# Residual rows kept in DRAM, and a second standing buffer for modulation weights

## The chip, the cores and the metric

The kernel runs on one core of a Trainium2 chip. A core has a matrix engine (TensorE, PE in the profile), a vector engine (VectorE, DVE), a scalar engine (ScalarE, ACT), a general engine (GpSimd, POOL) and SyncE (SP), which here issues nearly all the DMAs; 16 DMA engines move data between DRAM and the core's SBUF memory of 128 partitions. Each engine runs its own list of instructions in order and waits on semaphores for the others. The metric is the device time of one execution in microseconds, as a median of runs.

## The reference

One inference step of a small flow-matching backbone: 384 tokens (128 of context, 256 latent) by 1024 channels go through four layers. Layer `l` has the mixer `l mod 3`: a bidirectional state-space scan (SSD) in layers 0 and 3, a gated short convolution in layer 1, differential attention in layer 2. Each mixer and each conv-FFN (1024 to 5632, gated to 2816, back to 1024) stands between two norms, and its result is added to the residual `x`:

```
def sandwich_layer(x, mod, g, mix_fn, ffn_fn):
    sh1, sc1, gt1, sh2, sc2, gt2 = jnp.split(mod, 6, axis=-1)
    m, aux = mix_fn(rmsnorm(x, g[0]) * (1 + sc1) + sh1)
    x = x + gt1 * rmsnorm(m, g[1])
    f = ffn_fn(rmsnorm(x, g[2]) * (1 + sc2) + sh2)
    x = x + gt2 * rmsnorm(f, g[3])
    return x, aux
```

`mod` is `silu(c) @ w_mod[l]` plus a bias, with one vector `c` for latent and one for context tokens, and a `w_mod[l]` of 24 MB in each layer. The result is float32; the kernel splits each factor of its large products into a high and a low part and makes three matmuls of each.

## The kernel before

**Phases.** The program is unrolled. For each layer: the mixer, with activations held channel-major (channels on partitions); the mixer's output projection, token-major, in `tm_out`; the FFN's up projection (L374 holds the matmuls of all channel-major projections) with convolution and gate; the FFN's down projection, again in `tm_out` (matmuls at L414). A `tm_out` makes three row tiles of 128 tokens (t0, t1, t2), and works in two halves of 512 output columns. At the end of its second half each row tile is finished in turn: `gated` takes the projection times its gate, `residual` (L355) adds it to `x`, `normed` makes `xn`, `turned` transposes it on PE (L291), and `modulated` makes `hh` and `hl`, which the next phase's matmuls read. That end is called a turn here; there are eight: A and B behind mixer and FFN of layer 0, C and D of layer 1, E and F of layer 2, G and H of layer 3. In a turn PE has little left to do but transposes, and the chain goes through DVE, ACT and POOL for each row tile.

**Residual.** `x` is three tiles of 128 x 1024 float32 (512 KB each, 4 KB of a partition), in a pool of their own (`xp`), loaded once at the start by `tokens` and updated in place.

**Modulation.** The product with `w_mod` is cut into 24 units a layer, 96 in all. A unit loads a block of 1 MB and runs matmuls of it into `modps` (L184); eight units end in `mod_finish`, which adds the bias row `brow` on DVE (L194, L195), transposes (L198) and, for the gates, stores them to DRAM (`gd`). Units are fill work: `pace` puts them into all phases by a table of how many are to be done by when, and `need` forces those that a phase reads. Their blocks lie in `wm`, a standing buffer (`WM` of them) in the weights' pool, and in `wx`, of which `room` many lie in a phase's own pool: 7 at the start, 4 in the turns of the short convolution and of attention, 1 in the other `tm_out`, 0 elsewhere. `stock` issues the loads for all free buffers, `modbuf` picks the buffer, and `fill` runs units:

```
    def fill(self, n, stock=99):
        for _ in range(n):
            if self.filler:
                self.stock(stock)
                self.filler.pop(0)[1](self.modraw.pop(0)[0])
```

**Other loads.** Weights come in chunks of 512 KB (`wr`, 4 buffers), are split by ACT and DVE into `wh` and `wl` (4 buffers), and are thus some chunks ahead of PE. `gates` (L63 in the trace) reads a gate back from `gd`, spread over all partitions, at the middle of a `tm_out`.

**Order.** The Tile framework schedules the instructions of each engine statically, with a simulated timeline, and sets the semaphores. All loads and stores named here go through SP in one order; a DMA whose buffer isn't free, or whose source isn't ready, holds those behind it. DMAs rotate over eight semaphores, so that one waits for the eighth before it. A pool that is opened for a phase takes the memory of the phase before, and its tiles wait for the readers of what lay there.

Of the kernel before, what the change touches and what calls it, by code (L numbers as in the profile page):

```python
# [10 lines left out]
F32 = mybir.dt.float32  # L11
# [8 lines left out]
P = 128  # L20
D = 1024
KB = D // P
# [4 lines left out]
NF = FFN // P  # L27
# [4 lines left out]
EPS = 1e-6  # L32
# [3 lines left out]
WS = 4  # L36
WM = 1
RB = 7
# [6 lines left out]
class Net:  # L45
    def __init__(self, ctx, tc, d, layers):
        self.tc, self.nc, self.d, self.layers = tc, tc.nc, d, layers
        pool = lambda name, bufs=1, **kw: ctx.enter_context(tc.tile_pool(name=name, bufs=bufs, **kw))
        self.cp = pool("const")
        self.xp = pool("x")  # L50
        self.hp = pool("h")
        self.wp = pool("w", 3)
        self.mp = pool("mod", 1)
        self.sm = pool("small", 4)
        self.dp = pool("dram", 1, space=DRAM)
        self.pt = pool("pt", 2, space=PSUM)
        self.pm = pool("pm", 1, space=PSUM)
        self.V, self.S, self.GP, self.PE = self.nc.vector, self.nc.scalar, self.nc.gpsimd, self.nc.tensor
        self.consts()
# [42 lines left out]
    def tokens(self, lo, hi):  # L102
        d = self.d
        for t in range(lo, hi):
            xt = self.xp.tile([P, D], F32, name=f"x{t}")
            self.load(xt, d["x_prompt"] if t == 0 else d["x_sample"][(t - 1) * P:t * P, :])
            self.x.append(xt)

# [245 lines left out]

    def residual(self, t, parts, eps=EPS):  # L355

        r = self.rstd(parts[t, 0][1], parts[t, 1][1], eps)
        out = []
        for hf, xs in enumerate(self.halves(self.x[t])):
            self.V.scalar_tensor_tensor(xs, parts[t, hf][0], r, xs, op0=ALU.mult, op1=ALU.add)  # L360
            out.append(self.sums(xs))
        return out

# [21 lines left out]
    def tm_out(self, *args, room, **kw):  # L385

        with self.tc.tile_pool(name="out", bufs=1, reuse_waits="tile") as self.op:
            self.room, self.hbufs = room, HB
            self.stock()
            self._tm_out(*args, **kw)  # L390
            self.room = 0

    def _tm_out(self, l, gate, nk, prep, eps=None, then=None):
        self.goal["turn"] = self.goal["mid"] if gate == 0 else self.goal["end"]
        self.need(l, gate + 1)
        parts = {}
        self.limit = self.wpos + nk
        for hf in range(2):
# [6 lines left out]
            for k, t in order:  # L405
# [9 lines left out]
                if hf == 1 and k == nk - 1:  # L415
                    self.gated(t, 1, acc[t], gt, parts)
                    ss = self.residual(t, parts, EPS if eps is None else eps[t])
                    then(t, ss)
                    self.pace("turn", t + 1, NT)
# [23 lines left out]
    def run(self):  # L443
        tc = self.tc
        self.modres, self.filler, self.modraw, self.room = {}, [], [], 0
        self.x = []
        self.wplan = [c for l in self.layers for c in self.plan(l)]
# [47 lines left out]
    def ffn(self, l, pl, then):  # L495
        d = self.d
# [20 lines left out]

        self.tm_out(l, 1, NF, prep, then=then, room=1)

    def short(self, l, pl, then):  # L520
        d = self.d
# [5 lines left out]
        for i in range(KB):  # L527
# [7 lines left out]
            t = self.conv(cg, cw[:, i])  # L535
            self.V.tensor_tensor(t, pb, t, op=ALU.mult)
            self.split(t, hi[i], lo[i])
            self.pace("mix", i + 1, KB)
        self.tm_out(l, 0, KB, lambda k: (hi[k], lo[k]), then=then, room=4)

    def ssd(self, l, pl, then):
# [26 lines left out]

        self.tm_out(l, 0, 16, prep, eps=eps, then=then, room=1)

# [231 lines left out]
    def attn(self, l, pl, then):  # L802
        oh = [pl.tile([P, 2, T], F32R, name=f"oh{i}") for i in range(4)]
        ol = [pl.tile([P, 2, T], F32R, name=f"ol{i}") for i in range(4)]
        with self.tc.tile_pool(name=f"heads{l}", bufs=1, reuse_waits="tile") as hp:
            self.attn_core(l, hp, oh, ol)
        self.tm_out(l, 0, KB, lambda k: (oh[k // 2][:, k % 2, :], ol[k // 2][:, k % 2, :]), then=then, room=4)

# [250 lines left out]
```

## Time and profile before

| | us |
|---|---|
| median of 3 runs | 2415.24 (2411.56 to 2415.72) |
| the profiled execution | 2410.85 |
| its span | 2409.03 |
| PE busy | 2291.4 (95%) |
| DVE busy | 1613.2 (67%) |
| ACT busy | 1248.5 (52%) |
| DMA, mean share of its 16 engines | 48.8% |
| mean clock granted to PE | 0.975 |

A time of the trace counts from the start of the span. The granted clock is a share of 2.4 GHz: 1.0 or, at its lower level of 1.2 GHz, 0.5; a value between is a mean over a stretch. The stages, from the windows of the trace: start 0 to 43, mixer of layer 0 to 343, its projection and turn A to 437, FFN of layer 0 to 626, turn B to 733, layer 1's mixer to 845, turn C to 901, FFN to 1084, turn D to 1191, attention to 1346, turn E to 1444, FFN to 1629, turn F to 1737, layer 3's mixer to 2039, turn G to 2124, FFN to 2310, turn H to the end.

### The profile page before, as it was taken

The page shows a single profiled execution, that of the slowest core. Times are in us where ns is not written, and L with a number is a line of the kernel's source. Part 1 is how long each engine was busy: PE and PEld are TensorE (multiplying, and loading weights), DVE is VectorE, ACT ScalarE, POOL GpSimd, SP SyncE. Part 2 cuts the span into 40 slices and gives each one's busy share as a digit, 9 for nine tenths or more (in the row PEclk, how much of TensorE's full clock was granted, in tenths as well). Part 3 has the DMA queues.
Part 4 walks back from the last instruction along what each step waited for, and adds up shares of the span by engine and source line. Part 5 has one row for each costly group of instructions (what it writes and reads, how often), then busy time and mean ns, then how long its engine had stood idle before and what let it go on. Part 6 is the DMA issues. An engine that isn't in the chain of part 4 may idle for free.

```text
span 2409.0 us, 35648 instructions
## 1 busy us (share of the span) xinstructions
PE 2291.4 (95%) x13132; PEld 2001.4 (83%) x13132; DVE 1613.2 (67%) x2928; ACT 1248.5 (52%) x2165; POOL 330.0 (14%) x498
## 2 busy tenths in 40 slices
PE   6989999899999999999999979999898999989998
PEld 3878887799877959998788649998687888789987
DVE  3888786677655467776645547776578888677765
ACT  3766675444453344445544444445566676554444
POOL 1222221100000010000223320000113223110000
PEclk8999999999999999999999989999999999989999
DMA  7665655533547563335434453344465654423342
GB/s 293 188 173 206 213 189 177 201 123 124 165 135 292 194 246 116 131 123 164 157 123 153 153 236 109 131 129 157 141 171 168 190 178 143 131 98 125 130 147 80
DMA packets 113375, 391.79 MB, mean 163 GB/s; under 512 B 13105, under 2 KB 25521, under 8 KB 100913
## 3 DMA queue, kind: packets, MB, share of 16 engines
q1 hardware_dynamic: 113200, 389.52, 48.8%
q8 instruction: 103, 1.69, 0.3%
q14 instruction: 72, 0.58, 0.1%
HBM read 382.39 MB, written 7.08 MB: 162 GB/s over the span
## 4 chain that ended last, share of the span: by engine, by line
PE 81%; DVE 8%; DMA 4%; issue 2%; ACT 2%; POOL 2%; SPq 0%; DVEq 0%; POOLq 0%; ACTq 0%
PE mm L374 46%; PE mm L414 20%; PE mm L846 5%; PE modps L184 3%; PE yp L414 2%; DVE e L719 2%; PE yp L759 2%; DMA wm<-in_w_mod 1%; DVE wl L153 1%; PE yp L887 1%; DVE w L723 1%; DMA h<-in_state 1%; DMA wx<-in_w_mod 1%; PE yp L374 1%; ACT jk L260 1%
## 5 line engine op out<-in xcount | busy, mean ns | idle before, releaser
L374 PE MATMUL mm<-hh,wh 128*128 128x384 f32 (+1 forms) x2352 | 795.9, 340 | 11.3 <-DVE cv L434 7.4
L374 PE MATMUL mm<-hl,wh 128*128 128x384 f32 (+1 forms) x2352 | 794.7, 338 | 1.8 <-POOL hl L346 1.8
L374 PE MATMUL mm<-hh,wl 128*128 128x384 f32 (+1 forms) x2352 | 791.5, 338 | 0.0
L153 DVE TENSOR_TENSOR wl<-wr,wh 128x1024 fp32r<-128x1024 f32 (+2 forms) x466 | 564.9, 1214 | 278.6 <-ACT wh L152 277.9
L152 ACT ACTIVATE wh<-wr 128x1024 fp32r<-128x1024 f32 (+2 forms) x466 | 483.4, 1039 | 340.7 <-PE mm L374 261.6
L374 PEld LDWEIGHTS mm<-hh,wh 128*128 128x128 f32 (+1 forms) x2352 | 442.7, 189 | 37.3 <-DVE cv L434 11.4
L374 PEld LDWEIGHTS mm<-hl,wh 128*128 128x128 f32 (+1 forms) x2352 | 442.6, 188 | 5.8 <-POOL hl L346 2.3
L374 PEld LDWEIGHTS mm<-hh,wl 128*128 128x128 f32 (+1 forms) x2352 | 442.4, 188 | 5.0 <-issue 3.1
L430 ACT ACTIVATE cv<-mm,fcw 128x384 f32<-128x384 f32 x176 | 100.1, 571 | 233.3 <-PE mm L374 228.2
L414 PE MATMUL mm<-wh,gh 128*128 128x512 f32 x528 | 208.7, 395 | 0.0
L414 PE MATMUL mm<-wl,gh 128*128 128x512 f32 x528 | 208.6, 395 | 0.0
L414 PE MATMUL mm<-wh,gl 128*128 128x512 f32 x528 | 207.9, 395 | 0.0
L432 DVE SCALAR_TENSOR_TENSOR cv<-mm,fcw,cv 128x127 f32<-128x127 f32 x352 | 144.3, 411 | 42.5 <-ACT cv L430 42.5
L439 ACT ACTIVATE gh<-fg 128x384 fp32r<-128x384 f32 x176 | 92.2, 524 | 152.5 <-PE mm L414 151.6
L268 POOL TENSOR_SCALAR m<-s 128x1 f32<-128x1 f32 x42 | 17.1, 406 | 1123.3 <-ACT jk L260 1122.4
L440 DVE TENSOR_TENSOR gl<-fg,gh 128x384 fp32r<-128x384 f32 x176 | 97.6, 557 | 96.7 <-ACT gh L439 96.1
L434 DVE SCALAR_TENSOR_TENSOR cv<-mm,fcw,cv 128x127 f32<-128x127 f32 x352 | 146.0, 416 | 10.9
L414 PEld LDWEIGHTS mm<-wh,gh 128*128 128x128 f32 x528 | 99.0, 187 | 24.7 <-issue 0.8
L414 PEld LDWEIGHTS mm<-wh,gl 128*128 128x128 f32 x528 | 99.0, 187 | 24.4
L414 PEld LDWEIGHTS mm<-wl,gh 128*128 128x128 f32 x528 | 99.0, 187 | 24.0
L184 PE MATMUL modps<-wm,sil 128*32 128x512 f32 x496 | 75.1, 646 | 13.9 <-DMA wm<-in_w_mod 12.9
L846 PE MATMUL mm<-wh,hh 128*128 128x256 f32 x288 | 83.4, 290 | 0.0
(235 smaller groups left out, 3149.7 us busy)
## 6 DMA issues: line engine op xcount, KB each, us to landing
wr<-in_ffn_up SPq DMA_DIRECT2D x176, 512.0 KB
wm<-in_w_mod SPq DMA_DIRECT2D x62, 1024.0 KB
wr<-in_ssd_in SPq DMA_DIRECT2D x96, 512.0 KB
wr<-in_ffn_down SPq DMA_DIRECT2D x88, 512.0 KB
wx<-in_w_mod SPq DMA_DIRECT2D x34, 1024.0 KB
ab<-acs SPq DMA_DIRECT2D x48, 512.0 KB
wr<-in_ssd_out SPq DMA_DIRECT2D x32, 512.0 KB
wr<-in_sc_in SPq DMA_DIRECT2D x32, 384.0 KB
```

What stands on the lines that cost most here:

```text
L152: self.S.activation(hi[:, :m], raw[:, :m], AF.Copy)
L153: self.V.tensor_tensor(lo[:, :m], raw[:, :m], hi[:, :m].bitcast(F32), op=ALU.subtract)
L184: self.PE.matmul(acc[32 * j:32 * j + 32, :], self.sil[:, kb, :], raws[:, j // 2, (j % 2) * 512:(j % 2 + 1) * 512], start=kb == 0, stop=kb ...
L374: self.PE.matmul(acc[:m], w, h, start=n == 0, stop=n == len(ops) - 1)
L414: self.PE.matmul(acc[t], g[:, o:o + n], w, start=k == 0 and i == 0, stop=k == nk - 1 and i == 2)
L430: self.S.activation(t, src, AF.Copy, scale=cw[:, 1:2])
L432: self.V.scalar_tensor_tensor(t[:, o + 1:o + n], src[:, o:o + n - 1], cw[:, 0:1], t[:, o + 1:o + n], op0=ALU.mult, op1=ALU.add)
L434: self.V.scalar_tensor_tensor(t[:, o:o + n - 1], src[:, o + 1:o + n], cw[:, 2:3], t[:, o:o + n - 1], op0=ALU.mult, op1=ALU.add)
L439: self.S.activation(hi, src, AF.Copy)
L440: self.V.tensor_sub(lo, src, hi.bitcast(F32))
L719: V.scalar_tensor_tensor(e[:, sl], abs_[t][:, 0, sl], dac[:, t, hs:hs + 1], abs_[t][:, 1, sl], op0=ALU.subtract, op1=ALU.min)
L846: PE.matmul(acc[t][:, :256], h[k][:, o:o + m], w[:, ws], start=k == 0 and i == 0, stop=k == KB - 1 and i == 2)
```

## The change

Three things change together.

1. `WM` goes from 1 to 2: a second standing `wm` of 8 KB of each partition.
2. The pool of `x` (12 KB of a partition) goes. `x` now lives in DRAM: the inputs at first, and then a fresh tile per layer, gate and row tile. `rows` loads the three row tiles at the start of every `tm_out`, behind `stock`, into the phase's pool; `residual` stores a row tile when it is updated (but for the last, which goes to the output as before). That is 24 loads beside the first three, and 21 stores, of 512 KB.
3. `room` goes from 4 to 3 in the turns of short convolution and attention, and from 1 to 0 in the others, so that a `tm_out` has as many buffers of modulation weights as before (5 or 2). At the start `room` stays 7, and eight blocks are loaded as before: two `wm` and six `wx`.

```
-WM = 1
+WM = 2
...
-        self.xp = pool("x")
...
     def tokens(self, lo, hi):
         d = self.d
         for t in range(lo, hi):
-            xt = self.xp.tile([P, D], F32, name=f"x{t}")
-            self.load(xt, d["x_prompt"] if t == 0 else d["x_sample"][(t - 1) * P:t * P, :])
-            self.x.append(xt)
+            self.xd.append(d["x_prompt"] if t == 0 else d["x_sample"][(t - 1) * P:t * P, :])
+        self.rows()
+
+    def rows(self):
+
+        self.x = []
+        for t, src in enumerate(self.xd):
+            self.x.append(self.op.tile([P, D], F32, name=f"x{t}"))
+            self.load(self.x[t], src)
...
-    def residual(self, t, parts, eps=EPS):
+    def residual(self, l, gate, t, parts, eps=EPS):
...
+        if not (l == self.layers[-1] and gate == 1):
+            self.xd[t] = self.dp.tile([P, D], F32, name=f"xd{l}{gate}{t}")
+            self.nc.sync.dma_start(self.xd[t], self.x[t])
         return out
...
             self.room, self.hbufs = room, HB
             self.stock()
+            self.rows()
             self._tm_out(*args, **kw)
...
-                    ss = self.residual(t, parts, EPS if eps is None else eps[t])
+                    ss = self.residual(l, gate, t, parts, EPS if eps is None else eps[t])
...
-        self.tm_out(l, 1, NF, prep, then=then, room=1)
+        self.tm_out(l, 1, NF, prep, then=then, room=0)
...
-        self.tm_out(l, 0, KB, lambda k: (hi[k], lo[k]), then=then, room=4)
+        self.tm_out(l, 0, KB, lambda k: (hi[k], lo[k]), then=then, room=3)
...
-        self.tm_out(l, 0, 16, prep, eps=eps, then=then, room=1)
+        self.tm_out(l, 0, 16, prep, eps=eps, then=then, room=0)
```

The schedule moves with it. Three places show how; each is given before and after, a row being line, operation, output and inputs, shape, and how often in a row.

PE in the mixer of layer 0, around 122 to 137 us of the trace, before: `modps` are the units (x4 is one unit), `yp<-w,xt` the scan's products that need DVE's `w`, `sp` a product for the next state.

```order
L374 MATMUL mm<-hh_249,wl 128x384
L184 MATMUL modps<-wm,sil 32x512 x4
L759 MATMUL yp<-w,xt 64x128 x4
L184 MATMUL modps<-wm,sil 32x512 x4
L759 MATMUL yp<-w,xt 64x128 x4
L759 MATMUL yp<-ab,h_1011 64x128 x4
L759 MATMUL yp<-ab,s 64x128 x4
L374 MATMUL mm<-hh_248,wh 128x384
```

The same place after:

```order
L382 MATMUL mm<-hh_246,wl 128x384
L189 MATMUL modps<-wm,sil 32x512 x4
L750 MATMUL sp<-xw,bt 128x256 x2
L189 MATMUL modps<-wm,sil 32x512 x8
L768 MATMUL yp<-w,xt 64x128 x4
L189 MATMUL modps<-wm,sil 32x512 x4
L768 MATMUL yp<-w,xt 64x128 x4
L768 MATMUL yp<-ab,h_1010 64x128 x4
L768 MATMUL yp<-ab,s 64x128 x4
L382 MATMUL mm<-hh_245,wh 128x384
```

Four units stand where two stood; the second and third are together, ahead of the first `yp<-w,xt`, and the fourth ahead of the second one.

PE in turn B, before, from the transposes of row tile 0 to the first matmuls of the next mixer; `tp<-ident,xn` and `mm<-ident,xn` are the transposes of the row tiles:

```order
L414 MATMUL mm<-wh,gl 128x512
L291 MATMUL tp<-ident,xn 128x128 x8
L184 MATMUL modps<-wx,sil 32x512 x4
L291 MATMUL mm<-ident,xn 128x128 x8
L184 MATMUL modps<-wm,sil 32x512 x4
L291 MATMUL tp<-ident,xn 128x128 x8
L184 MATMUL modps<-wx,sil 32x512 x4
L184 MATMUL modps<-wm,sil 32x512 x4
L374 MATMUL mm<-hh_6737,wh 128x384 x3
```

Turn B after, the same stretch:

```order
L296 MATMUL tp<-ident,xn 128x128 x8
L189 MATMUL modps<-wm,sil 32x512 x4
L423 MATMUL mm<-wh,gl 128x512
L423 MATMUL mm<-wh,gh 128x512
L423 MATMUL mm<-wl,gh 128x512
L423 MATMUL mm<-wh,gl 128x512
L189 MATMUL modps<-wm,sil 32x512 x4
L296 MATMUL mm<-ident,xn 128x128 x8
L189 MATMUL modps<-wm,sil 32x512 x8
L296 MATMUL tp<-ident,xn 128x128 x8
L382 MATMUL mm<-hh_6754,wh 128x384 x3
L189 MATMUL modps<-wm,sil 32x512 x4
```

Two units that stood behind the transposes of row tile 2 stand ahead of them now.

SP in turn D, before: the last weight chunks of the down projection, then those of attention (`in_qkv`) and the reloads of modulation weights.

```order
L63 DMA wr<-in_ffn_down 128x1024 x14
L63 DMA wr<-in_qkv 128x1024 x6
L63 DMA wx<-in_w_mod 128x2048
L63 DMA wr<-in_qkv 128x1024
L63 DMA wm<-in_w_mod 128x2048
L63 DMA wr<-in_qkv 128x1024
L63 DMA wm<-in_w_mod 128x2048
L63 DMA cs<-in_rot 128x256
```

SP in turn D, after; `xd` is a row tile's place in DRAM:

```order
L62 DMA wr<-in_ffn_down 128x1024 x13
L62 DMA wr<-in_qkv 128x1024 x5
L369 DMA xd_10861<-x_10155 128x1024
L369 DMA xd_10946<-x_10157 128x1024
L62 DMA wr<-in_qkv 128x1024
L62 DMA wm<-in_w_mod 128x2048
L62 DMA wr<-in_qkv 128x1024
L62 DMA wm<-in_w_mod 128x2048
L62 DMA wr<-in_qkv 128x1024
L369 DMA xd_11028<-x_10159 128x1024
L62 DMA wm<-in_w_mod 128x2048 x2
L62 DMA cs<-in_rot 128x256
```

The stores of row tiles 0 and 1 stand ahead of the first reload, that of row tile 2 behind the second.

## Rows read from the trace of the kernel before

**Rows 1.** Page's head: span, busy time of each engine, what the DMA moved.

```profile
span 2409.0 us, 35648 instructions
...
PE 2291.4 (95%) x13132; PEld 2001.4 (83%) x13132; DVE 1613.2 (67%) x2928; ACT 1248.5 (52%) x2165; POOL 330.0 (14%) x498
...
DMA packets 113375, 391.79 MB, mean 163 GB/s; under 512 B 13105, under 2 KB 25521, under 8 KB 100913
```

**Rows 2.** Windows: stretch, length, busy us (count) PE PEld DVE ACT POOL, clock, DMA, GB/s.

```profile
43.00:343.00 300.00, 285.41 (x1887) 253.98 (x1888) 236.98 (x489) 197.62 (x329) 80.58 (x86) 0.98 0.59 188
...
1346.00:1444.00 98.00, 80.07 (x403) 49.57 (x400) 45.65 (x84) 42.70 (x117) 28.50 (x65) 0.89 0.54 203
```

**Rows 3.** What PE waited for: us in all, times, longest.

```profile
PE modps L184 <- DMA wx<-in_w_mod: 18.0, 9, 4.7
...
PE modps L184 <- DMA wm<-in_w_mod: 12.9, 7, 3.4
```

**Rows 4.** Timeline of PE, layer 0's mixer: start, length, instruction, idle before it.

```profile
43.07 0.58 PE L374 MATMUL mm<-hl,wh 128*64 128x384 f32 x1 [1.79 <-POOL hl L346]
...
78.41 1.07 PE L184 MATMUL modps<-wm,sil 128*32 128x512 f32 x8 [1.66 <-DMA wm<-in_w_mod]
...
129.48 1.12 PE L759 MATMUL yp<-w,xt 128*64 128x128 f32 x8 [5.70 <-DVE w L724]
...
133.34 1.93 PE L184 MATMUL modps<-wm,sil 128*32 128x512 f32 x8 [2.74 <-DMA wm<-in_w_mod]
```

**Rows 5.** Chain of waits: start, length, what (near 126 us, and turn E).

```profile
126.05 7.24 DMA wm<-in_w_mod
...
1405.32 12.82 DMA gate<-gd
```

**Rows 6.** Tile h, 60 to 200 us: its engines' idle time until, us, times.

```profile
  DMA h<-in_state: 5.7, 1
```

**Rows 7.** Timeline of PE, layer 3's mixer.

```profile
1770.62 1.45 PE L184 MATMUL modps<-wm,sil 128*32 128x512 f32 x8 [2.06 <-DMA wm<-in_w_mod]
...
1829.42 1.93 PE L184 MATMUL modps<-wm,sil 128*32 128x512 f32 x8 [2.21 <-DMA wm<-in_w_mod]
```

**Rows 8.** Windows, columns as in rows 2, two stretches of layer 3's mixer.

```profile
1771.00:1775.00 4.00, 4.00 (x18) 3.01 (x11) 2.99 (x8) 2.76 (x5) 0.00 (x0) 0.57 0.42 131
...
1822.00:1832.60 10.60, 4.30 (x28) 2.27 (x30) 10.60 (x31) 4.37 (x9) 1.04 (x1) 0.52 0.55 177
```

**Rows 9.** Timeline of PE, turns and one unit of an FFN.

```profile
433.06 1.97 PE L291 MATMUL tp<-ident,xn 128*128 128x128 f32 x8 [7.27 <-DVE xn L281]
...
460.55 1.07 PE L184 MATMUL modps<-wm,sil 128*32 128x512 f32 x8 [0.88 <-DVE brow L194]
...
728.53 1.94 PE L291 MATMUL tp<-ident,xn 128*128 128x128 f32 x8 [4.29 <-DVE xn L281]
...
894.16 3.49 PE L184 MATMUL modps<-wx,sil 128*32 128x512 f32 x16 [2.80 <-DVE brow L194]
...
1185.63 1.93 PE L184 MATMUL modps<-wx,sil 128*32 128x512 f32 x8 [4.35 <-DMA wx<-in_w_mod]
...
1187.53 1.94 PE L291 MATMUL tp<-ident,xn 128*128 128x128 f32 x8
...
1191.13 0.39 PE L846 MATMUL mm<-wh,hh 128*128 128x256 f32 x1
...
1730.06 1.84 PE L184 MATMUL modps<-wx,sil 128*32 128x512 f32 x8 [4.68 <-DMA wx<-in_w_mod]
```

**Rows 10.** Timeline of DVE, turn D: the residual's update.

```profile
1170.42 1.42 DVE L360 SCALAR_TENSOR_TENSOR x<-rt,r,x 128x512 f32<-128x512 f32 x2 [0.38 <-POOL r L270]
...
1181.78 1.40 DVE L360 SCALAR_TENSOR_TENSOR x<-rt,r,x 128x512 f32<-128x512 f32 x2
```

**Rows 11.** Timeline of SP, turn D: a reload's issue.

```profile
1178.05 0.33 SPq L63 DMA_DIRECT2D wx<-in_w_mod  x1
```

**Rows 12.** DMA, 0 to 30 us: rate in 40 slices.

```profile
GB/s 0 0 150 109 213 404 339 404 426 384 457 426 426 448 404 459 371 459 415 404 459 382 492 360 426 448 382 481 360 448 426 393 470 382 459 393 366 355 393 421
```

More of the change, by code (lines that the diff above doesn't have):

```diff
@@ L445, in run @@
         self.modres, self.filler, self.modraw, self.room = {}, [], [], 0
-        self.x = []
+        self.xd = []
         self.wplan = [c for l in self.layers for c in self.plan(l)]
@@ L806, in attn @@
             self.attn_core(l, hp, oh, ol)
-        self.tm_out(l, 0, KB, lambda k: (oh[k // 2][:, k % 2, :], ol[k // 2][:, k % 2, :]), then=then, room=4)
+        self.tm_out(l, 0, KB, lambda k: (oh[k // 2][:, k % 2, :], ol[k // 2][:, k % 2, :]), then=then, room=3)
     def attn_core(self, l, pl, oh, ol):
```

## The prediction

> **What bounds the kernel now.** I read the page's head first, then the windows by stage, then what TensorE (PE) waited for, and only then single places. The reader sees PE busy for 2291.4 of 2409.0 us [rows 1]: everything the change can win by removing waits lies in the 118 us left. The windows say where they lie: a mixer of layer 0 loses 15 us of 300 and the attention turn E loses 18 of 98 at a granted clock of 0.89 [rows 2]. The waits say for what: 18.0 us for `wx` and 12.9 us for `wm`, both blocks of modulation weights [rows 3]. Nine of the wx waits are spread over the start, where eight units load at the full DMA rate whatever their buffers are, and over the turns. So what a second standing buffer can reach is well under 31 us, and the sum has to be made place by place.
>
> The times below come from the profiled execution: span 2409.03 us, 2410.85 us with what lies around it. The median of the runs is 2415.24, so 4.4 us above it; I make the sum against the profiled run and carry the difference to the median.
>
> **What the change removes.** A unit costs PE about 1.07 us at full clock [rows 4]; all 96 are still done, so only idle time and low clock count.
>
> *Mixer of layer 0.* PE's wait of 1.79 us for POOL at 43.07 gets a second unit put into it: 1.05. The unit at 78.41 waited 1.66 us for its reload; two units stand together now and both are loaded: 1.66 [rows 4]. One reload less stands ahead of the scan's states `h`, for which POOL idled 5.7 us once [rows 6]; a reload is 1 MB, which at some 420 GB/s [rows 12] is 2.5 us, so an estimate between 0 and 2.5; POOL is not the bound there, I take 1. Around 130 the change puts four units where two stood (first excerpt). There PE waits 5.70 us for `w` at 129.48, then 2.74 for a reload [rows 4]. That reload took 7.24 us from 126.05 [rows 5], since SP holds it behind the store of a state. Units one and two of the four are loaded; the third needs the same reload at the same time and now stands ahead of the `yp` group, not behind it; the fourth is one reload (2.5 us) later. So the group ends 1.5 to 2.5 us later than now, with two more units (2.1 us) done: 0, between -2 and +1. Sum 3.7.
>
> *Turn A.* Two units (2.1 us) move behind the last matmul of row tile 2, whose chain through DVE ends the turn: PE waits 7.27 us for its `xn` at 433.06 [rows 9]. DVE may be the limit of that chain: 0 to 2.1, taken 1.0. *FFN of layer 0:* it holds no unit any more, and the 0.88 us wait at 460.55 [rows 9] goes: 0.9. *Turn C:* 2.80 us of waiting for `brow` [rows 9], with fewer units in that group: 0 to 2.8, taken 1.0.
>
> *Mixer of layer 3.* The wait of 2.06 us at 1770.62 goes [rows 7], and the low clock after it: 4.00 us of work at 0.57 [rows 8] is 1.7 us too long. That is 3.7. Here the four units around 1820 are split: two ahead of the wait for `w`, two behind the `yp` groups, so that the second pair's reload runs under DVE's work. The wait of 2.21 at 1829.42 [rows 7] stays, but two more units fit: -2 to +2, taken 1. `h` as above: 1. Sum 5.7. Turns G and H hold no units: 0.
>
> Removed in all: 3.7 + 1.0 + 0.9 + 1.0 + 5.7 = 12.3 us.
>
> **What the change adds.** 24 loads and 21 stores of 512 KB, each 1.25 us of the DMA at its full rate [rows 12], all on SP's one queue. The arithmetic of `x` is the same. The loads stand at the start of an output projection, behind the stock and ahead of the gates. Their cover: the gates are needed half a projection later, and the weights are split several chunks ahead; if that cover went, three loads would cost 3.75 us. In one place it isn't there: *turn E*, where the gates are late already: 12.82 us from issue [rows 5], behind four `wx` (4 MB). After, three `wx` and three `x` (4.5 MB) stand there: 1.3 us at the rate of [rows 12], and everything behind it is one chain through DVE. Bounds 0 (the landing of the third `wx` is earlier) and 3; taken 1.3.
>
> The stores stand in the turns, each waiting on SP for DVE's `x`, with reloads and weight loads queued behind it. *Turn D* is the clearest (third excerpt). Row tile 0 is ready at 1170.42 + 1.42, in a pause of the DMA, and tile 2 only at 1181.78 [rows 10]; tile 1 comes between them, so its 0.5 MB is partly in flight when the first reload is issued at 1178.05 [rows 11]. That reload lands at 1185.6 now [rows 9] and 0 to 1.3 us later after; unit and transposes of tile 2 follow, and the next mixer's first matmul 3.6 us behind these (1187.53 to 1191.13 [rows 9]). That the reload is `wm` and not `wx` gains nothing, since one unit comes first in both orders. 0.7, and one unit (1.07) that ran under the last chain is done elsewhere, half of it in waits: 1.2, between 0 and 2.5. *Turn F* has the same wait, 4.68 at 1730.06 [rows 9]: 0.9, 0 to 2. *Turn B:* before, two units stood behind tile 2's transposes and ran under the chain to the next matmul; now they stand ahead of them (second excerpt), on reloads that are issued only when the two units before have run. PE waits there 4.29 us for `xn` at 728.53 anyway [rows 9]; I expect the second of them about 2 us past that, of which 0.8 is won back behind, as no unit follows: 1.2, between 0 and 3. In A the stores find the same reloads earlier, and DVE's chain covers them: 0.
>
> Added in all: 1.3 + 1.2 + 0.9 + 1.2 = 4.6 us. Net 12.3 - 4.6 = 7.7: 2403.2 for a run like the profiled one, **2407.5** against the median.
>
> **The rivals.** *No change:* the second buffer doesn't do what it is there for, because both reloads follow each other through one queue, and the groups of four units wait for the second pair. Then the two groups cost 2 each, `h`, A and C bring nothing: 1.05 + 1.66 + 0.9 + 3.7 - 4 - 4.6 = -1.3, that is about 2416. For it: a reload takes 7.24 us, not 2.5 [rows 5], and PE idles on DVE there anyway, 5.70 us [rows 4]. Against it: only two of the places have four units.
>
> *Slower:* the stores. One mechanism: in a turn the reloads that PE waits for are issued behind the three stores of the same turn. Three stores are 3.75 us; in A, B, D, E and F that is 18.8, less 12.3 won, 6.5 slower: 2421.7. It decides from 2.5 us a turn, two stores of three ahead of the reload. For it: the DMA runs full in these turns' ends, so that 1 MB took 7.5 us [rows 9, 11]. Against it: tile 0's store finds an idle DMA and tile 2's comes after the issue of the reloads [rows 10, 11]. The Trainium skill's page Perfetto Trace Analysis, section DMA Optimizations, advises giving loads and stores different issuing engines; this change puts its stores among the loads, and by that advice this is the rival to fear. No run here shows it yet.
>
> *Faster still:* the clock comes back with the waits. Around 1822 to 1832.6 PE did 4.30 us of work at 0.52 [rows 8], and the unit at 133.34 took 1.93 instead of 1.07 [rows 4]: 2.1 us in each mixer's group if it ran at full clock, 4.2 in all; with turns that lose nothing, 2407.5 - 4.2 - 4.6 = 2398.7. Against it: the 5.70 us before it are DVE's, and idle stays idle. The Trainium skill's page TensorE: Matmul & The Clock Gate, section HAM oscillation, says that waits for DMA throw the array back to its lower clock; the rows agree for 1770.62, and by that rule each removed wait would bring this extra.
>
> **How the numbers follow.** Forecast 0.50, no change 0.28, slower 0.15, faster still 0.07. A measurement here tells about 0.2% (4.8 us) from no change, so the bound for faster is 2410.4. The forecast lies beyond it by 2.9, and six in seven of its cases do: 0.43 + 0.07 + 0.02 of the no-change case make 0.52; same 0.31; slower 0.17. The range: all low ends together give 2422, all high ends 2394; both need every place to fall one way, so 2398 to 2421.
>
> **What would show it.** Right: no wait for `wm` at 78 and 1770, no `wm` wait over 1 us in the mixers but the third unit of the group near 130, which stands ahead of `yp`; windows of both mixers 3 to 6 us shorter; B, D, E and F each about a microsecond longer, with waits for `wm` where `wx` stood. Wrong: mixers no shorter (the groups wait); a turn more than 2.5 us longer with SP held at a store; PE waiting for `wr`, which would mean that the traffic itself, 45 x 0.5 = 22.5 MB on 391.8 [rows 1], reaches the matmuls.

## The result and the profile after

The changed kernel is slower: 2426.56 us (2424.16 to 2430.19) against 2415.06 (2411.56 to 2415.72), a ratio of 1.006 with an interval of 1.0048 to 1.0071. The profiled execution took 2424.44 us with a span of 2422.7, 13.7 more than before.

The page's head after, for [rows 1]:

```profile
span 2422.7 us, 35709 instructions
...
PE 2304.0 (95%) x13132; PEld 2010.3 (83%) x13132; DVE 1611.7 (67%) x2928; ACT 1241.4 (51%) x2159; POOL 327.8 (14%) x498
...
DMA packets 119854, 415.38 MB, mean 171 GB/s; under 512 B 13824, under 2 KB 26240, under 8 KB 107392
```

PE is busy 12.6 us longer with the same 13132 matmuls, and idle only 1.1 us longer (118.7 for 117.6). So the reader should not look for new waits alone. About half of the 12.6 is more work and half a lower clock, as the table of the experiments shows below. Cut by phase (a phase ends at the first matmul of the next in PE's timeline, attention's mixer at the first matmul of its output projection's second half), before, after, and three experiments told below:

| us | before | after | e5 | e10 | e11 |
|---|---|---|---|---|---|
| start, mixer 0, turn A | 437.6 | 430.5 | 435.1 | 430.9 | 439.7 |
| FFN 0, turn B | 296.2 | 296.1 | 296.7 | 296.1 | 295.7 |
| short convolution, turn C | 167.4 | 172.2 | 166.8 | 172.9 | 169.3 |
| FFN 1, turn D | 289.9 | 289.4 | 289.2 | 291.3 | 290.0 |
| attention's mixer | 195.6 | 208.5 | 188.7 | 183.3 | 183.2 |
| turn E | 57.4 | 57.4 | 56.0 | 57.4 | 59.0 |
| FFN 2, turn F | 291.9 | 292.2 | 292.2 | 292.0 | 290.7 |
| mixer 3, turn G | 388.2 | 392.4 | 388.4 | 393.7 | 387.0 |
| FFN 3, turn H | 284.8 | 283.9 | 284.9 | 284.5 | 283.3 |
| span | 2409.0 | 2422.7 | 2398.1 | 2402.1 | 2397.9 |

The gain at the start is there, and larger than forecast. It is lost in the short convolution (4.8), in attention's mixer (12.9) and in the mixer of layer 3 (4.2). What PE waited for after, for [rows 3] (us in all, times, longest):

```profile
PE modps L189 <- DMA wm<-in_w_mod: 30.6, 9, 9.3
...
PE mm L382 <- DVE cv L443: 8.6, 6, 1.8
PE modps L189 <- DMA wx<-in_w_mod: 6.8, 6, 1.9
PE yp L768 <- DVE w L733: 6.5, 4, 2.2
```

The waits for modulation weights change their name, from wx 18.0 and wm 12.9 to wm 30.6 and wx 6.8: 6.5 us more in all.

**Attention's mixer** shows that waits for modulation weights are not the cause there. Windows (columns as in [rows 2]) of before, up to the output projection's first matmuls, and the rest:

```profile
1191.10:1346.00 154.90, 154.90 (x1145) 130.99 (x1141) 79.80 (x173) 72.19 (x188) 49.28 (x116) 1.00 0.43 143
1346.00:1386.70 40.70, 37.63 (x179) 24.50 (x177) 20.56 (x43) 19.42 (x59) 13.56 (x39) 0.87 0.45 154
```

The same of after:

```profile
1188.20:1351.50 163.30, 163.30 (x1158) 133.58 (x1154) 80.22 (x172) 72.28 (x187) 44.46 (x114) 1.00 0.46 152
1351.50:1396.70 45.20, 39.38 (x174) 26.73 (x171) 19.73 (x43) 19.12 (x60) 14.39 (x41) 0.81 0.37 126
```

The first stretch is 8.4 us longer with PE busy all of it, at full clock, in both. So PE had more to do there. What, two timelines tell. (The second stretch, called the tail here, is 4.5 us longer by idle time and clock.) PE before, one unit whole and a quarter of one (a matmul counts two in the x of these rows, so x8 is a unit):

```profile
844.09 1.06 PE L184 MATMUL modps<-wm,sil 128*32 128x512 f32 x8
...
869.74 1.04 PE L184 MATMUL modps<-wm,sil 128*32 128x512 f32 x2
```

PE after, in the short convolution, pieces of one and a quarter, one and three quarters, and a quarter:

```profile
771.14 1.90 PE L189 MATMUL modps<-wm,sil 128*32 128x512 f32 x10
...
785.66 1.92 PE L189 MATMUL modps<-wm,sil 128*32 128x512 f32 x14
...
829.72 1.04 PE L189 MATMUL modps<-wm,sil 128*32 128x512 f32 x2
```

One matmul of a unit takes 1.04 us and four take 1.06: the four, each on 32 columns of PE's array, run side by side. Five take 1.90, as seven do. A unit that the planner (the Tile framework's scheduling, which fixes PE's order) cuts in two pays twice, once in each place. Call each such run of up to four a pass. Counted in PE's order, before makes 101 passes for its 96 units and after 108. (The expectation of e4 has 109. It counts two where the last quarter of one unit and three of the next stand together at 846.1 us; these take 1.06 us, one pass.) Extra passes by cuts are 3 more in short convolution with turn C, 3 more in attention's mixer and 1 more in the mixer of layer 3. Besides, two units changed their phase: one went from turn B to layer 1, one from layer 3's mixer to attention's.

Attention has a second kind. Its score matmuls (`kT,qT`) use 64 of the array's 128 rows, two to a row tile and head pair. Before, alone:

```profile
1245.01 0.91 PE L887 MATMUL yp<-kT,qT 64*128 64x384 f32 x2
```

And in the experiment e9, where two are kept together:

```profile
1231.79 0.92 PE L903 MATMUL yp<-kT,qT 64*128 64x384 f32 x4
```

Two together cost what one does alone. The 48 of them make 36 passes before and 41 after; all five more are in the first stretch. The groups of the lines' view (busy us, mean ns) of before:

```profile
L887 PE MATMUL yp<-kT,qT 64*128 64x384 f32 x64 | 26.7, 561 | 1.1 <-ACT p L893 1.1
L887 PE MATMUL yp<-kT,qT 64*128 64x128 f32 x32 | 4.9, 323 | 0.0
```

and of after, 3.7 us more for the same matmuls:

```profile
L896 PE MATMUL yp<-kT,qT 64*128 64x384 f32 x64 | 28.9, 570 | 2.1 <-ACT p L902 2.1
L896 PE MATMUL yp<-kT,qT 64*128 64x128 f32 x32 | 6.4, 364 | 0.0
```

The Trainium skill's page TensorEngine Tiling (Array Packing), section Key Properties, says that tiles of the array operate independently, and that a change of tiling mode drains the engine. The first is what these rows show for neighbours in the queue. That a matmul of the whole array between two of them ends it, the rows show too (0.91 us each apart, 0.92 for both together), and it fits the second; no row shows the drain by itself.

**The mixer of layer 3.** PE before, where a single unit stands ahead of a convolution that DVE finishes late, at two of five such places:

```profile
1871.27 1.07 PE L184 MATMUL modps<-wm,sil 128*32 128x512 f32 x8
1873.15 0.44 PE L374 MATMUL mm<-hh,wh 128*128 128x384 f32 x1 [0.81 <-DVE cv L434]
...
1906.57 1.06 PE L184 MATMUL modps<-wm,sil 128*32 128x512 f32 x8
1908.44 0.44 PE L374 MATMUL mm<-hh,wh 128*128 128x384 f32 x1 [0.81 <-DVE cv L434]
```

After, the last two units are a pair, and the later places have none:

```profile
1882.00 1.92 PE L189 MATMUL modps<-wm,sil 128*32 128x512 f32 x16
1884.61 0.44 PE L382 MATMUL mm<-hh,wh 128*128 128x384 f32 x1 [0.69 <-DVE cv L443]
...
1919.87 0.44 PE L382 MATMUL mm<-hh,wh 128*128 128x384 f32 x1 [1.80 <-DVE cv L443]
...
1956.76 0.44 PE L382 MATMUL mm<-hh,wh 128*128 128x384 f32 x1 [1.80 <-DVE cv L443]
```

Without its unit PE waits 1.80 us for 0.81, at four places (the others are at 1992.08 and 2028.96). Behind two of the four it runs the next matmuls at a lower clock. The windows behind the first two, after:

```profile
1919.87:1925.90 6.03, 6.03 (x26) 5.78 (x28) 4.60 (x8) 3.82 (x6) 0.00 (x0) 0.72 0.84 238
1956.76:1961.20 4.44, 4.44 (x26) 4.19 (x27) 4.41 (x8) 3.82 (x6) 0.00 (x0) 1.00 0.85 225
```

and before, behind the wait of 0.81 at 1873.15:

```profile
1873.15:1877.58 4.43, 4.43 (x26) 4.18 (x28) 4.39 (x8) 3.83 (x6) 0.00 (x0) 1.00 0.83 173
```

The same 26 matmuls take 6.03 us at a mean clock of 0.72 and 4.43 at 1.00; it is 0.72 again behind 1992.08 and 1.00 behind 2028.96. So a unit of 1.06 us in such a place covered 1.0 of waiting, four times, and was free there; at two of the places its going cost 1.6 of clock besides. Why the clock fell at only two of four equal waits isn't shown.

### The profile page after: what moved, and what is told of

Its sections match the earlier page's. It is cut to its first block, busy times and chain, and to the rows that moved or that the text cites. A ratio compares the mean times of both kernels' runs of the same rounds, so it can differ in the third digit from the quotient of the medians.

```text
span 2422.7 us, 35709 instructions
## 1 busy us (share of the span) xinstructions
PE 2304.0 (95%) x13132; PEld 2010.3 (83%) x13132; DVE 1611.7 (67%) x2928; ACT 1241.4 (51%) x2159; POOL 327.8 (14%) x498
## 4 chain that ended last, share of the span: by engine, by line
PE 82%; DVE 7%; DMA 4%; ACT 2%; issue 2%; POOL 2%; SPq 0%; POOLq 0%; ACTq 0%; DVEq 0%
PE mm L382 46%; PE mm L423 21%; PE mm L855 5%; PE modps L189 3%; PE yp L423 2%; DVE e L728 2%; PE yp L768 2%; DMA wm<-in_w_mod 2%; PE yp L896 1%; DVE wl L158 1%; DMA h<-in_state 1%; DVE w L732 1%; PE yp L382 1%; DMA wx<-in_w_mod 1%; ACT jk L265 1%
## 5 line engine op out<-in xcount | busy, mean ns | idle before, releaser
L189 PE MATMUL modps<-wm,sil 128*32 128x512 f32 x624 | 100.5, 668 | 30.7 <-DMA wm<-in_w_mod 30.6
```

What stands on the lines that cost most here:

```text
L189: self.PE.matmul(acc[32 * j:32 * j + 32, :], self.sil[:, kb, :], raws[:, j // 2, (j % 2) * 512:(j % 2 + 1) * 512], start=kb == 0, stop=kb ...
```

## The experiments

To compare the kernels, PE's time from 30 us on is cut in three, by windows of 2 us: idle; lost to the clock (busy time times one minus the granted clock); and the rest, its work at full clock. "Passes" are counted in PE's order: units, and scores. Ratios are to the kernel before, whose median beside the experiments was 2411.8 to 2412.6.

| kernel | unit, score passes | idle | clock | work | median | ratio |
|---|---|---|---|---|---|---|
| before | 101, 36 | 103.3 | 35.5 | 2240.2 | | 1 |
| after | 108, 41 | 104.3 | 41.7 | 2246.7 | 2426.56 | 1.006 |
| e1 rows only | 103, 38 | 108.6 | 40.8 | 2244.9 | 2431.02 | 1.0069 |
| e2 one late | 105, 41 | 105.5 | 36.2 | 2245.6 | 2424.07 | 1.0039 |
| e3 no stores | 109, 39 | 101.3 | 39.8 | 2247.3 | 2418.77 | 1.0025 |
| e4 after, whole units | 96, 41 | 109.7 | 49.1 | 2236.7 | 2425.81 | 1.0055 |
| e5 before, whole units | 96, 34 | 101.8 | 33.1 | 2233.3 | 2403.65 | 0.9973 |
| e6 rows only, whole | 96, 40 | 104.8 | 39.3 | 2239.4 | 2420.76 | 1.0033 |
| e7 whole, no stores | 96, 43 | 108.2 | 37.2 | 2239.3 | 2420.7 | 1.0035 |
| e8 before, pairs | 96, 24 | 112.5 | 39.8 | 2224.6 | 2408.34 | 0.9986 |
| e9 rows only, pairs | 96, 24 | 107.2 | 47.1 | 2221.9 | 2405.75 | 0.9972 |
| e10 after, pairs | 96, 24 | 112.4 | 38.7 | 2221.0 | 2406.3 | 0.9978 |
| e11 rows only, loads late | 96, 24 | 108.8 | 36.5 | 2222.6 | 2398.7 | 0.9946 |
| e12 after, loads late | 96, 24 | 110.2 | 41.4 | 2220.0 | 2403.68 | 0.9971 |
| e13 one late, loads late | 96, 24 | 107.4 | 38.6 | 2222.3 | 2400.08 | 0.9954 |
| e14 pairs, no stores | 96, 24 | 110.3 | 45.3 | 2218.3 | 2402.0 | 0.996 |
| e15 stores by ACT | 96, 24 | 116.5 | 46.7 | 2221.7 | 2413.0 | 1.0006 |
| e16 stores by POOL | 96, 24 | 119.3 | 46.1 | 2224.0 | 2417.92 | 1.0021 |

The column of work follows the passes: 137 passes 2240, 149 passes 2247, 130 passes 2233, 120 passes 2218 to 2225. What it doesn't tell is in the other two: of the 13.7 us between before and after, work is 6.5, clock 6.2 and idle time 1.0.

### One part alone: e1, e2, e3

e1 takes the second buffer away and leaves the rows in DRAM:

```
-WM = 2
+WM = 1
...
-        self.tm_out(l, 1, NF, prep, then=then, room=0)
+        self.tm_out(l, 1, NF, prep, then=then, room=1)
...
```

> The changed kernel with one standing buffer again (WM 1, room 4 and 1 as before), the residual rows still in DRAM: the traffic and its place in the queue alone. Theory A (the second buffer is the loss: the schedule runs units earlier and in pairs, so that none is left for the gaps at the end of attention and in the late groups of layer 3's mixer): between 2411 and 2420, attention and layer 3's mixer as long as before, turns up to 2 us longer each. Theory B (the rows are the loss: 45 DMAs of 512 KB in SP's queue hold the loads of weights and gates): 2422 to 2430.

e2 fills only one of the two standing buffers outside the output projections of layers 2 and 3:

```
-        for pool, tag, bufs in ((self.wp, "wm", WM), (self.op, "wx", self.room)):
+        for pool, tag, bufs in ((self.wp, "wm", 1), (self.wp, "wm2", self.wmn - 1), (self.op, "wx", self.room)):
...
+            self.late = n > 1
+            self.wmn = 1 if self.late else WM
```

> The changed kernel, but in layers 2 and 3 only one of the two standing buffers is filled outside the output projections, so that the units of attention and of layer 3's mixer run singly and spread as before. The rows stay in DRAM. Theory A: layer 3's mixer wins back 4 to 7 us and attention 3 to 10, so 2409 to 2419. Theory B: the traffic is the same, so 2423 to 2429.

e3 drops the stores, and every output projection loads the input rows, so that its result lacks the residual sum:

```
-            self.xd[t] = self.dp.tile([P, D], F32, name=f"xd{l}{gate}{t}")
-            self.nc.sync.dma_start(self.xd[t], self.x[t])
+            pass
```

> The changed kernel without the 21 stores: every output projection loads the rows of the input again, so the residual sum is left out of the result; instructions on the compute engines are the same. Theory A: 2421 to 2427, a turn wins 0 to 1.5 us. Theory B: 2412 to 2420, turns B, D, E and F each 2 to 3 us shorter.

Measured: 2431.02 (1.0054 to 1.0084), 2424.07 (1.0025 to 1.0052), 2418.77 (1.0015 to 1.0035). e1 is slower than either theory gave. The rows alone cost 15 us of span, so the loss doesn't need the second buffer. With it, the start is 7.0 us and turn E 4.2 shorter than in e1 (437.5 and 61.6 there), and attention's mixer 8.7 longer (199.8 there). e2's time is theory B's, yet it brings mixer 3 with turn G from 392.4 back to 388.8, near what theory A said, with waits for `cv` of 0.80 at four of five places again; that settles the lost fill there. Attention stays at 206.3. e3's time is theory B's too, but not its places: turns B, D, E and F are no shorter. Without stores the kernel was 8 us faster, with 8.7 in attention's mixer (199.8 for 208.5), in which no store stands. Its passes are about as many (109, 39); the 8.7 is idle time and clock, most of it in the tail. That gap between cause and place, and PE's full busy time in the first stretch, led to the passes.

### Whole units: e4 to e7

The last three matmuls of a unit are queued behind the first with priority, so that nothing comes between. e4 is that in after, e5 in before, e6 in e1, e7 in e3:

```
-            for j in range(4):
-                self.PE.matmul(acc[32 * j:32 * j + 32, :], self.sil[:, kb, :],
...
+            def quarter(j):
+                return self.PE.matmul(acc[32 * j:32 * j + 32, :], self.sil[:, kb, :],
...
+            first = quarter(0)
+            with self.tc.issue_after(getattr(first, "ins", first)), self.tc.high_priority():
+                for j in range(1, 4):
+                    quarter(j)
```

> The changed kernel with the four matmuls of a unit kept together in PE's order (the last three are queued right behind the first). In the trace a unit's four matmuls take 1.06 us together (x8 in the rows), and one of them alone 1.04 (x2): they run side by side. A unit that is cut in two therefore pays twice. Counted in PE's order, before makes 101 such passes for its 96 units, after 109. Theory P (passes): after loses 13 passes of 0.93 us each, 12 us, so 2412 to 2415, at or near before; the pitch between chunks in the short convolution falls from 14.5 to 14.5 only where two whole units stand, but the mixer-and-turn-C segment falls from 172 to about 168, attention from 201 to about 198. Theory R (the rows' transfers): cut units are an accident of bookkeeping, time stays 2421 to 2427.

> The kernel before with the four matmuls of a unit kept together; else its PE order is the same up to a few places. Theory P: 5 passes of 0.93 us go, 4.7 us faster than before, ratio 0.998. Theory R says nothing on it: 1.000.

> Rows in DRAM with one standing buffer (as in the run with rows only), units whole. Theory P: 7 passes less than that run, 6.5 us less: 2424 to 2425, and the rest against the whole-unit kernel before is what the rows themselves cost, some 12 us; Theory R: 2429 to 2432, no gain from whole units, all of the loss is the rows'.

> The changed kernel with whole units and without the 21 stores of rows: each output projection loads the input rows (the residual sum is left out). Without stores and with cut units it was 6 to 8 us faster than after, but its PE order in attention differed too. Here PE's order is that of the whole-unit after in nearly all places. Theory R (the stores hold SP's queue in front of reloads): 6 to 8 us below the whole-unit after. Theory O (the earlier gain was the order, not the stores): within 2 us of it.

e5: 2403.65, 0.9973 (0.996 to 0.9986), 8.2 us below before by the medians and 6.5 by the ratio, where 4.7 was expected; its work fell by 6.9, for 5 unit passes and 2 score passes. e6: 2420.76, 10 below e1, where 6.5 was expected; its span is 10.7 shorter, 5.5 of that work. Both kernels keep the order of their neighbours nearly everywhere, and both show that a cut unit costs its pass. e4 is a miss of the time: 2425.81, no better than after. Its work fell by 10.0 (12 expected), but the clock took 7.4 of it and idle time 5.4: whole units find their places earlier, 15 in the short convolution (12 in after), 8 in attention's mixer (11), and none late in the mixer of layer 3, as in after. That the places they left became waits is likely, not shown place by place; in the short convolution with turn C PE is idle 6.7 us for 3.7. So undoing the cuts alone does not give the changed kernel its time back. e7 is 5.1 us below e4, between the two theories.

### Whole pairs of scores: e8 to e10

The first score matmul waits until the second's PSUM bank is free too, and the second follows it. e8 is that in e5, e9 in e6, e10 in e4:

```
-                for e in range(2):
-                    sp = self.psum("yp")[:, :w]
-                    PE.matmul(sp, qT[64 * e:64 * e + 64, dh, t * P:(t + 1) * P], kT[64 * e:64 * e + 64, dh, ks], start=True, stop=True)
-                    ps.append(sp)
+                ps = [self.psum("yp")[:, :w] for e in range(2)]
...
+                first = score(0)
+                if self.freed is not None:
+                    self.tc.add_manual_dep(first, self.freed.name, mybir.DependencyInfo(mybir.DependencyClass.Sync, mybir.DependencyReason.DATA), reason="pair")
+                with self.tc.issue_after(first), self.tc.high_priority():
+                    score(1)
```

> The whole-unit kernel before, and in attention the two score matmuls of a head pair (64 rows of the array each) kept together too: the first waits until the second's PSUM bank is free as well. In the trace two of them queued together take 0.92 us (x4 in the rows), one alone 0.91 (x2), at 384 columns; 0.49 and 0.48 at 128. In PE's order the 48 score matmuls make 34 passes in the whole-unit before, 24 here: 8 passes of 0.84 and 2 of 0.42 less. Theory P (parts of PE's array run side by side only when queued together): 7.6 us faster than the whole-unit before, 2396. Rival T (attention's tail is a chain of waits, and a score that waits for two banks is later there): 2401 to 2406.

> The same for rows in DRAM with one buffer and whole units: score passes 40 to 24, 12 of 0.84 and 4 of 0.42 less. Theory P: 11.8 us faster than the run with rows and whole units, 2409, and the cost of the rows (against the kernel before made in the same way) falls from 17 to about 13. Rival T: 2415 to 2420.

> The same for the changed kernel (rows and two buffers), units whole: score passes 41 to 24, 12 of 0.84 and 5 of 0.42 less. Theory P: 12 us faster than the whole-unit after, 2413 to 2414. Rival T: 2420 to 2426. That whole units alone gained nothing there (2425.8 for 2424.5) is a miss of theory P so far, unless the gain was lost in the mixer segments.

Measured: e8 2408.34, 4.7 above e5, and later than rival T gave too; e9 2405.75, 15 below e6, and e10 2406.3, 19.5 below e4, both more than theory P gave. The work fell in all three (8.7, 17.5 and 15.7). In e9 the score groups of the lines' view are:

```profile
L903 PE MATMUL yp<-kT,qT 64*128 64x384 f32 x64 | 15.4, 559 | 1.2 <-ACT p L915 1.1
L903 PE MATMUL yp<-kT,qT 64*128 64x128 f32 x32 | 3.9, 323 | 0.0
```

19.3 us for 31.6 before. Attention's mixer takes 183.2 us in e9 and 183.3 in e10, with rows in DRAM, and 193.7 in e8 without. Windows of e8, the cut here 4 us behind the output projection's first matmul:

```profile
1190.50:1345.00 154.50, 150.08 (x1176) 130.81 (x1173) 82.73 (x177) 71.06 (x189) 46.87 (x116) 1.00 0.49 160
1345.00:1384.20 39.20, 31.32 (x147) 21.73 (x146) 16.75 (x40) 18.28 (x57) 13.79 (x39) 0.83 0.26 92
```

There PE waits 12.3 us in both stretches together, where e5 waits 3.5, and the tail's clock is 0.83 for 1.00. A likely reason, not shown: what stood between two scores hid the softmax behind the first. In e9 and e10 the same pairs stand, with units and projections at other places, and the loss is smaller.

With nothing cut, the changed kernel (e10) and the kernel before (e8) are 0.08% apart, and the changed one is ahead of the kernel before as it was: 0.9978 (0.9967 to 0.9989). Part of that is e8's own loss at its tail: against e5 e10 is 2.7 us behind.

### Where the rows are loaded, and the second buffer again: e11 to e13

e11 is e9 with the row loads behind the gates; e12 is the same in e10, and e13 in e10 with e2's one late buffer:

```
             self.stock()
-            self.rows()
...
                 gt = self.gates(l, gate)
+                self.rows()
```

> The kernel with rows, one buffer, whole units and pairs, with the three row loads moved from the start of the output projection behind the loads of the gates. In turn E of the run with rows and whole units the first gated product waits 2.2 us longer and the clock loss is 9.1 us for 3.6 in the same kernel without rows. Theory L (row loads in front of the gates make turn E late): 4 to 6 us faster than its neighbour with the loads in front, all of it in turn E. Rival (the loads are hidden, it is the stores): within 1.5 us.

> The changed kernel (two standing buffers, rows in DRAM), units whole, scores in pairs, row loads behind the gates. Its neighbour with one buffer ran 2398.7. Theory W (the second buffer keeps its 7 us of mixer of layer 0 and turn A, and loses no more than it did in the short convolution and the mixer of layer 3): 2396 to 2399, no better than one buffer by more than 3. Theory B (the second buffer is worth what it wins at the start, 7 to 9 us, now that nothing is cut): 2390 to 2392. Theory N (late units are worth more than a standing buffer): 2401 to 2404.

> As the last one, but outside the output projections of layers 2 and 3 only one of the two standing buffers is filled, so that single units are left for the mixer of layer 3. Theory W: the mixer of layer 3 falls from 392 to 394 to about 388, 4 us below its neighbour with two buffers, about 2393. Theory N the same. If it comes out level with its neighbour, single units there are not worth what the run with one late buffer gave (4 us).

e11: 2398.7, 0.9946 (0.9929 to 0.9963), the fastest of all, 7 us below e9, where 4 to 6 was expected. Only 2.2 of it came in turn E (61.2 to 59.0); 5.0 came in the mixer of layer 3, where e9 waits:

```profile
1787.92 1.32 PE L756 MATMUL sp<-xw,bt 128*128 128x256 f32 x4 [3.79 <-POOL xw L755]
```

and e11:

```profile
1783.87 0.70 PE L756 MATMUL sp<-xw,bt 128*128 128x256 f32 x2 [1.53 <-POOL xw L755]
```

e12, with the second buffer, is 5.0 us slower than e11 (theory N), though their intervals touch (0.9959 to 0.9983 for e12): it wins 9.8 at the start and turn A and 4.0 in turn E, and gives back 3.4 in short convolution and turn C, 3.0 in attention's mixer, 2.8 in FFN 2 and turn F, 5.3 in the mixer of layer 3. e13 takes back 3.6, as expected in size, but not in place: 1.1 in mixer 3 and 3.5 in turn D. Once nothing is cut and the loads stand late, the second buffer costs more than it wins here. In turn E, late loads did what theory L said in both orders: PE's wait for the first gated product (`rt`), 2.4 us in e9 and 1.7 in e10, is gone in e11 and e12, and the turn is 2.2 and 2.4 shorter.

### The stores: e14 to e16

e14 is e10 without stores, as e3; e15 and e16 are e11 with the stores issued by ACT and by POOL:

```
-            self.nc.sync.dma_start(self.xd[t], self.x[t])
+            self.nc.scalar.dma_start(self.xd[t], self.x[t])
```

> The changed kernel with whole units and pairs, without the 21 stores of rows (each output projection loads the input rows; the residual sum is left out). Its neighbour with stores ran 2406.3. Theory S (the stores cost what the earlier runs without them suggest, 5 to 8 us): 2398 to 2401. Theory O (that was PE's order): 2404 to 2406.

> The kernel with one buffer, whole units, pairs and loads behind the gates (2398.7), with the 21 row stores issued by ACT instead of SP. Theory Q (the stores cost their 4 us by holding SP's queue in front of reloads): 2394 to 2396. Theory D (they cost DMA time, whoever issues them, or nothing): 2397 to 2401; later still if a store that waits for DVE holds ACT.

> The same with the row stores issued by POOL. Theory Q: 2394 to 2396. Theory D: 2397 to 2401; the units of attention stand one by one in nearly the same places as in the last one, so the two should agree within 2 us unless the issuing engine itself matters.

e14: 2402.0, 4.3 below e10, under the 5 to 8 of theory S; its profiled run is not shorter than e10's (2403.9 for 2402.1), so where the 4.3 lie isn't shown. e15 is 14.3 and e16 19.2 us slower than e11. Both theories gave less, D with "later still" left open. The work is the same (2221.7 and 2224.0 for 2222.6); idle time and clock took it, in attention's mixer (197.5 and 196.4 for 183.2) and the mixer of layer 3 (390.8 and 391.5 for 387.0). In the phases of the turns B, C, D, E and F, where stores stand, e15 is at most 0.7 us longer than e11, and e16 at most 1.1 but for 3.0 in FFN 0 and turn B. The planner had put attention's units elsewhere, one by one and early, and PE's waits for `on` at the tail of e15, of e11, and of e8, which has no row store at all, are

```profile
PE tp L944 <- DVE on L939: 8.5, 7, 2.3
...
PE tp L944 <- DVE on L939: 4.2, 2, 2.6
...
PE tp L935 <- DVE on L930: 8.5, 6, 2.6
```

So this wait comes without the stores too, with an order of PE that has a like tail. Whether the issuing engine costs anything by itself stays open, since the order moved with it; that SP's queue is what makes the stores dear is not borne out.

## Why the prediction was wrong

Forecast were 7.7 us less; measured are 11.5 more by the medians and 13.7 by the spans.

**Mixer of layer 0, turn A: right, and too small.** Forecast -4.7, measured -7.1. No wait stands at 43 and 78; the group around 130 went as described, its third unit behind its reload, 9.29 us for 5.70 and 2.74 before:

```profile
131.88 1.93 PE L189 MATMUL modps<-wm,sil 128*32 128x512 f32 x8 [9.29 <-DMA wm<-in_w_mod]
```

Turn A's wait for `xn`, 7.27 in [rows 9], is 4.95 after. The split between the two was not as forecast: the mixer ends only 1.8 us earlier (340.6 for 342.4), since three units of the projection moved into it, 26 for 23, and the projection with turn A is 5.3 shorter. The sign of mixers that are 3 to 6 us shorter did not come.

**FFN of layer 0 and turns B, D, F: no net cost.** The sum gave +0.3 for the first two together, +1.2 and +0.9 for D and F; measured, with the FFN ahead of each, -0.1, -0.5 and +0.3. In B that is luck in part: 5.2 us of waits for `wm` stand where 4.29 for `xn` stood, as forecast, and a unit less is run there. In D and F, waits for `wm` stand where `wx` stood, as forecast; in turn D:

```profile
1182.88 1.93 PE L189 MATMUL modps<-wm,sil 128*32 128x512 f32 x8 [4.11 <-DMA wm<-in_w_mod]
```

for 4.35 in [rows 9]. The stores ahead of it made it no longer.

**Turn E: right in kind, and offset.** Forecast +1.3, measured 0.0 (57.4 both). The gate lands after 13.07 us for 12.82 [rows 5], and PE has a new wait for the first gated product:

```profile
1430.18 0.79 PE L423 MATMUL mm<-wh,oh 128*128 128x512 f32 x1 [3.02 <-DVE rt L357]
```

Its waits for `wx` there fell from 4.19 to 1.86, and other terms made up the rest. Where four `wx` stand ahead of the rows, in e1, the turn takes 61.6.

**Turn C: wrong.** Forecast -1.0 for the turn and nothing for the convolution before it; measured +4.8. The wait of 2.80 for `brow` went, but one of 3.41 for `xn` stands in its place. The step that failed is the first sentence of the removals: "A unit costs PE about 1.07 us ... all 96 are still done, so only idle time and low clock count." A unit costs 1.07 whole, and near twice that in two pieces. With three more cuts and one unit more PE's work at full clock grew by 3.3 us here; the clock took 1.8, and idle time fell by 0.4.

**Attention: left out.** The mixer of layer 2 had no term in the sum, and no bound, since it holds no wait for modulation weights and PE is busy throughout. It lost 12.9 us. Of these 8.4 are in its first stretch: five more score passes (3.7 us), three more cuts, and two units more, one of them from its own tail. The other 4.5 are in the tail, where PE is idle 5.8 us for 3.1 and the mean clock 0.81 for 0.87. That is more than the whole sum of gains. For the passes the step that failed is the same one; for the tail it is the assumption under it, that a phase which the diff doesn't touch stays as it was. e3, with as many passes, has a tail 8.5 us shorter than after's, so the tail hangs on the order and not on the cuts. PE's order showed the cuts before any run: rows of x5 and x3, x7 and x1 where x4 stood.

**Mixer of layer 3: right at its start, wrong at its end.** The wait of 2.06 at 1770.62 went, as said. But the forecast's -5.7 is +4.2: single units that had stood under DVE's `cv` late in the phase were pulled into pairs, and four waits are 1.80 for 0.81. "Only idle time and low clock count" was right here, and the sum looked for them only where units wait, not where units hide waits. e2, which puts single units back there, recovers 3.6 of it.

**The rivals.** The faster side fell. No change had the right doubt, groups that wait for the second pair, and the wrong place. The rival of stores in front of reloads gave 2421.7, the nearest of all, but for the wrong reason: with 3.75 us more in each of five turns, of which none was longer by more than 0.3 with what stands ahead of it (A, B, D, F) or at all (E). Without stores the kernels ran 4 to 8 us faster (e3, e7, e14): in e3 all of it in attention's mixer, in e7 4.4 us there and 4.5 in the short convolution with turn C, in e14 not shown where; moving them to another queue, as the Trainium skill's page Perfetto Trace Analysis, section DMA Optimizations, would have it, brought no gain here (e15, e16). The rival of the clock was real with the other sign: the waits at 1919.87 and 1992.08 took clock as well. The Trainium skill's page TensorE: Matmul & The Clock Gate, section HAM oscillation, says that waits for DMA throw the array back to its lower clock. These are waits for DVE, and they agree in part: the window behind 1919.87 has 0.72, and the one behind 1956.76, after as long a wait, 1.00.

**The range** was too narrow for what it left out, rather than for what it counted: its bounds came from the places that were priced. It also stopped at 2421, below the time of its own rival of stores.

What stays open: why the planner cuts more with rows in DRAM. It plans with simulated times, and any new load moves those; that it is this, and not something particular in the rows, was only argued. No run kept PE's order and changed the DMA alone, so what the 45 transfers cost by themselves isn't separated from what the order costs. And e8's loss at attention's tail is shown as waits, but not which instruction there would have to move.

## What to carry to other kernels

Where matmuls use a part of PE's array and run side by side, count passes in PE's order before pricing anything else: a planner that puts one foreign matmul between them near doubles their cost, and no view calls that a wait. Keep such matmuls together by a dependency, and then see what they covered. Fill work has a price that depends on where it stands: late single units over another engine's latency are worth more than early pairs that only follow their loads.

## What the runs showed of the hardware

One matmul on 32 columns takes 1.04 us, four on different columns queued together 1.06, five 1.90; one score matmul on 64 rows 0.91, two on different rows 0.92. After four waits of 1.80 us PE ran the next 26 matmuls at a mean clock of 0.72 twice and of 1.00 twice; after one of 0.81 at 1.00. Six of the 45 added transfers run in turn D, and FFN 1 with turn D took 289.9 us before and 289.4 after: DMA traffic as such, 415.4 MB for 391.8 in all, did not slow PE there.
